# Preparing the down projection's weight factors: two raw tiles loaded a group in advance, two staging tiles

## The chip, the cores and the metric

The kernel runs on one core of a Trainium2 chip. The core has five engines that run side by side, each with its own queue of instructions that it works off in order: TensorE (PE; its weight loads, PEld, overlap its matmuls), VectorE (DVE), ScalarE (ACT), GpSimd (POOL) and SyncE (SP), which here issues nearly all DMAs. The metric is the time of one execution on the device in microseconds (us), the median of several runs.

## The reference, cut to what matters

One layer of a hybrid decoder over 1056 tokens (1024 of a prompt, 8 × 4 of samples): a norm, an input projection, two recurrent mixers (mLSTM and HGRN2) side by side, an output projection, and a SwiGLU feed-forward network with 1024 model columns and 2816 hidden ones (22 tiles of 128). All is float32.

```python
    x = x + jnp.einsum('btm,md->btd', mix, w_out)
    h2 = _rmsnorm(x, norm_ffn)
    ff = jax.nn.silu(jnp.einsum('btd,df->btf', h2, w_gate)) * jnp.einsum('btd,df->btf', h2, w_up)
    x = x + jnp.einsum('btf,fd->btd', ff, w_down)
```

The change is in how `w_down` (`wd` in the kernel) is made ready for the last line.

## The kernel before, in words

**Float32 products from rounded pieces.** TensorE multiplies rounded operands (type fp32r). So each operand is split in two: `hi` is the value rounded by a copy on ACT, `lo` is the value less `hi`, a subtraction on DVE or POOL. A product is three matmuls: hi·hi, hi·lo, lo·hi. Every weight and every activation goes through such a rounding on ACT before it can be used.

**Seven products in place of eight.** The gate-and-up stage and the down projection use Strassen's scheme in Winograd's form on 2 × 2 blocks, so sums and differences of weight blocks are formed, rounded and subtracted too.

**The stages.** Input projection with the mixers (to about 690 us), output projection and two of the 22 hidden tiles ("plain"), the gate-and-up stage over the other 20 hidden tiles (from about 760 to 1175 us, `g_step`, matmuls at L1228), the plain part of the down projection (L1492), the down projection (`d_step`, L1451), and the final norm.

**The weight preparation.** `wd_prep` runs beside the gate-and-up stage. It goes through 20 groups (`NG`); a group is a block of four hidden tiles by 256 model columns, 128 × 4 × 256 numbers, 512 KB. Per group it loads the raw block (`fload`, L1357) into the tile `fr`, which has one buffer, and makes four pieces of it. Per piece, `rnd` rounds on ACT (L1364) into the upper half of a staging tile `fh`, which has three buffers, and `rest` subtracts on DVE into its other half (L1369) and stores the whole tile to DRAM (`d_wf`, L1370): three pieces of 512 KB and one of 256 KB. Between the pieces four differences are formed on DVE in place in `fr` (L1383, L1385, L1388, L1390). The down projection later loads the finished factors from `d_wf` (`dload`, L1419); the stage's end waits for the preparation to be finished (`finish(("wd",))`).

**The order.** All queues are in the program's order, which the kernel writes out by hand. Side work is held in Python generators; `hook()` counts down each one's wait and, when it has come, lets it emit its next instructions up to its next `yield n`, which asks for n more hooks. In the gate-and-up stage a step is 24 matmuls (two halves of 12) and calls `hook()` four times. So a `yield 2` in `wd_prep` puts its next instructions two hooks, 12 matmuls, later into the queues of ACT, DVE and SP, between the work of the stage: the copies that empty PSUM on ACT (L1236, L1196), the sums on DVE (L1195, L1199, L1201), the splitting of the gate and up weights (L1145 on DVE, L1156 on ACT, L1157 on POOL), their loads (L1134) and the stores of results (L1209) on SP. An instruction that must wait for its data holds up all that stands behind it in its engine's queue.

**The hooks of one group before.** The three waits are `WDY = (2, 2, 5)`. With the group's first rounding at hook 0: second rounding and first store 2, second store 4, differences 6 and 8, third rounding and third difference 10, fourth difference 12, third store and fourth rounding 14, fourth store 16, load of the next group 18, next group's first rounding 23.

Of the kernel before, what the change touches and what calls it, by code (L numbers as in the profile page):

```python
# [9 lines left out]
F32 = mybir.dt.float32  # L10
F32R = mybir.dt.float32r
# [29 lines left out]
def hybrid_step(ctx: ExitStack, tc: tile.TileContext, i, o):  # L41
# [964 lines left out]
    fpool = [None]  # L1006
# [338 lines left out]
    NG = 4 * NS  # L1345
# [6 lines left out]
    def wd_prep():  # L1352

        def fload(g):
            t = fpool[0].tile([128, 4, 256], F32, tag="fr", name="fr", bufs=1)
            f = NPLAIN + 4 * (g // 4)
            nc.sync.dma_start(t, i["wd"].rearrange("(f p) d -> p f d", p=128)[:, f:f + 4, 256 * (g % 4):256 * (g % 4) + 256])  # L1357
            return t

        def rnd(src):  # L1360
            n = 128 * src.shape[1]
            t = fpool[0].tile([128, 1024], F32R, tag="fh", name="fh", bufs=3)
            h, lw = (x.rearrange("p (f c) -> p f c", c=128) for x in (t[:, 0:n], t[:, n:2 * n]))
            nc.scalar.activation(h, src, AF.Copy)  # L1364
            return t, h, lw, n

        def rest(g, k, src, p):
            t, h, lw, n = p
            nc.vector.tensor_tensor(lw, src, h.bitcast(F32), op=OP.subtract)  # L1369
            nc.sync.dma_start(d_wf[g, k, :, 0:2 * n], t[:, 0:2 * n].bitcast(F32))  # L1370
        r = fload(0)
        yield WDY[0]
        for g in range(NG):
            left, right = r[:, :, 0:128], r[:, :, 128:256]
            a11, a12, a21, a22 = left[:, 0:2], left[:, 2:4], right[:, 0:2], right[:, 2:4]
            p = rnd(left)
            yield WDY[1]
            rest(g, 0, left, p)
            p = rnd(a22)
            yield WDY[1]  # L1380
            rest(g, 1, a22, p)
            yield WDY[1]
            nc.vector.tensor_tensor(a22, a21, a22, op=OP.add)  # L1383
            yield WDY[1]
            nc.vector.tensor_tensor(a21, a11, a21, op=OP.subtract)  # L1385
            yield WDY[1]
            p = rnd(right)
            nc.vector.tensor_tensor(a11, a22, a11, op=OP.subtract)  # L1388
            yield WDY[1]
            nc.vector.tensor_tensor(a12, a12, a11, op=OP.subtract)  # L1390
            yield WDY[1]
            rest(g, 3, right, p)
            p = rnd(left)
            yield WDY[1]
            rest(g, 2, left, p)
            yield WDY[1]
            if g + 1 < NG:
                r = fload(g + 1)
            yield WDY[2]

    WDY = (2, 2, 5)

    def dplace(g, k):

# [283 lines left out]
    nxt = 2  # L1688
# [9 lines left out]
    for ui, u in enumerate(units + [None]):  # L1698
        if ui == units1:
            start(t3_prep(), ("t3",))  # L1700
            gi, TPK = 2, 2
            for k, (gu_, p) in enumerate(steps):
                while gi < len(groups) and gat[gi] <= k and (groups[gi][1] != 1 or (1, 0) in graw):
                    start(gsplit(*groups[gi], dve=gi < 2), ("gs", gi))
                    gi += 1
                finish(("gs", groups.index((GROUP[p], gu_))))
                if k == TPK:
                    finish(("t12",))
                if (gu_, p) == (0, "P7"):
                    finish(("tp",))  # L1710
                    finish(("t3",))
                if (gu_, p) == (1, "P1"):
                    start(wd_prep(), ("wd",))
                if (gu_, p) == (NU - 2, "P4"):
                    finish(("gs", len(groups) - 1))
                    start(plain_prep(), ("s2", 0))
                    hook()
                    load(n_t1)
                    load(n_t1 + 1)
                    for j in range(2):  # L1720
                        start(split(n_t1 + j, True), ("w", n_t1 + j), WLW[j])
                g_step(gu_, p)
                if (gu_, p) == (NU - 1, "P6"):
                    x2[0] = act.tile([128, KT, T], F32, tag="X", name="X2")
                    load_x2(0)
                    load_x2(2)
# [198 lines left out]
```

## Time and profile before

| | us |
|---|---|
| median of 3 runs | 1428.82 (1426.03 to 1429.61) |
| the profiled execution | 1429.1 |
| its span, first to last instruction | 1427.3 |
| mean granted TensorE clock | 0.98 |
| TensorE busy | 1363.0 |
| VectorE busy | 951.2 |
| GpSimd busy | 643.1 |
| ScalarE busy | 523.8 |
| bytes moved by DMA | 211.97 MB, 149 GB/s over the span |

The profile is one execution, in us from the start of its span. Rows of groups and timelines name an engine, a line of the kernel, an operation and its tiles as out<-in; in square brackets stands the time for which the engine had nothing running before that row, and what ended it. Rows of waits read "engine tile line <- what ended the wait: us in total, times, longest". Rows of windows give the busy time of each engine in a stretch with its number of instructions, then TensorE's granted clock as a share, the mean busy share of the 16 DMA engines, and GB/s. Rows of the chain give start, length and what, along the chain of work that ended last.

### The profile page before, as it was taken

What the parts mean: (1) busy time and instruction counts of PE and PEld (TensorE: products, weight loads), DVE (VectorE), ACT (ScalarE), POOL (GpSimd) and SP (SyncE); (2) the same over time, 40 slices, a digit from 0 to 9 for tenths busy, and PEclk for the clock granted to TensorE, in tenths of its full rate; (3) what the DMA queues carried; (4) which work ended last, traced back from release to release, by engine and by line L of the source; (5) the groups of instructions that cost most, each with busy time, mean ns of one, the idle gap of its engine ahead of it and who ended that gap; (6) DMA issues with size and microseconds to landing.
All of it is one profiled execution on the core that took longest, in us unless ns stands there. A gap on an engine that the chain in (4) does not pass through costs nothing. (4 is left out here: it accounts for less than half of the span.)

```text
span 1427.3 us, 27173 instructions
## 1 busy us (share of the span) xinstructions
PE 1363.0 (95%) x10384; PEld 1332.7 (93%) x10384; DVE 951.2 (67%) x2192; ACT 523.8 (37%) x1195; POOL 643.1 (45%) x648
## 2 busy tenths in 40 slices
PE   7878999999999999999998999999999999999996
PEld 6778999899999998899998999999999999999995
DVE  7876657666767677753756666665766436777776
ACT  6544334232222223322535444544444441222233
POOL 5323212234344434312537656655655684544445
PEclk8999999999999999999999999999999999999998
DMA  6012112331100113542463665665666268787843
GB/s 220 23 42 76 58 45 72 97 94 30 33 31 32 42 34 98 162 149 90 144 218 115 242 233 182 234 223 204 210 215 219 87 210 330 281 300 276 297 168 122
DMA packets 108875, 211.97 MB, mean 149 GB/s; under 512 B 10800, under 2 KB 63560, under 8 KB 108232
## 3 DMA queue, kind: packets, MB, share of 16 engines
q1 hardware_dynamic: 108312, 209.98, 43.0%
q8 instruction: 82, 1.34, 0.4%
q14 instruction: 49, 0.40, 0.1%
q10 hardware_dynamic: 432, 0.24, 0.1%
HBM read 143.73 MB, written 66.45 MB: 147 GB/s over the span
## 5 line engine op out<-in xcount | busy, mean ns | idle before, releaser
L135 PE MATMUL mm<-HI,whi 128*128 128x384 f32 (+2 forms) x1160 | 382.8, 330 | 5.4 <-ACT st L417 1.8
L137 PE MATMUL mm<-HI,wlo 128*128 128x384 f32 (+2 forms) x1160 | 363.5, 313 | 1.3 <-POOL wlo L97 1.3
L136 PE MATMUL mm<-LO,whi 128*128 128x384 f32 (+2 forms) x1160 | 363.9, 314 | 0.9 <-POOL LO L225 0.4
L135 PEld LDWEIGHTS mm<-HI,whi 128*128 128x128 f32 x1160 | 222.1, 191 | 10.7 <-ACT st L417 2.1
L136 PEld LDWEIGHTS mm<-LO,whi 128*128 128x128 f32 x1160 | 222.5, 192 | 2.1 <-POOL LO L225 0.9
L137 PEld LDWEIGHTS mm<-HI,wlo 128*128 128x128 f32 x1160 | 221.8, 191 | 1.8 <-POOL wlo L97 1.8
L97 POOL TENSOR_TENSOR wlo<-raw,whi 128x512 fp32r<-128x512 f32 x90 | 119.7, 1339 | 145.0 <-ACT whi L96 100.1
L1157 POOL TENSOR_TENSOR wlo<-S,whi 128x512 fp32r<-128x512 f32 x78 | 108.3, 1395 | 112.8 <-ACT whi L1156 95.9
L1369 DVE TENSOR_TENSOR fh<-fr,fh 128x512 fp32r<-128x512 f32 x80 | 77.3, 971 | 71.9 <-ACT fh L1364 71.3
L1228 PE MATMUL mx<-T,whi 128*128 128x264 f32 x640 | 118.5, 284 | 1.7 <-DVE sg L1195 1.7
L1228 PEld LDWEIGHTS mx<-T,whi 128*128 128x128 f32 x640 | 99.0, 188 | 2.0 <-DVE sg L1195 1.9
L1281 POOL TENSOR_TENSOR LO<-rg,HI 128x528 fp32r<-128x528 f32 x52 | 69.8, 1351 | 65.8 <-ACT HI L1280 59.5
L1228 PE MATMUL mx<-HI,whi 128*128 128x264 f32 x320 | 92.0, 287 | 4.4 <-ACT u L1236 4.4
L1228 PE MATMUL mx<-HI,wlo 128*128 128x264 f32 x320 | 91.6, 286 | 0.0
L1228 PE MATMUL mx<-LO,whi 128*128 128x264 f32 x320 | 91.4, 286 | 0.0
L1228 PE MATMUL mx<-T,wlo 128*128 128x264 f32 x320 | 90.9, 284 | 0.0
L802 POOL TENSOR_TENSOR ck<-ck,wib 128x192 f32<-128x192 f32 (+2 forms) x72 | 41.2, 572 | 100.5 <-PE mx L757 56.2
L1455 DVE TENSOR_TENSOR X<-X,mx 128x264 f32<-128x264 f32 x160 | 65.5, 425 | 26.4 <-PE mx L1451 26.0
L1156 ACT ACTIVATE whi<-S 128x512 fp32r<-128x512 f32 x80 | 50.4, 631 | 75.4 <-DVE S L1145 75.2
L1364 ACT ACTIVATE fh<-fr 128x512 fp32r<-128x512 f32 x80 | 45.2, 570 | 72.2 <-DMA fr<-in_wd 49.6
L1280 ACT ACTIVATE HI<-rg 128x528 fp32r<-128x528 f32 x52 | 32.3, 642 | 105.0 <-PE mx L1451 36.8
L1228 PE MATMUL mm<-HI,whi 128*128 128x264 f32 x240 | 68.3, 285 | 0.0
(536 smaller groups left out, 3604.0 us busy)
## 6 DMA issues: line engine op xcount, KB each, us to landing
d_wf<-fh SPq DMA_DIRECT2D x60, 512.0 KB
rg<-d_ff SPq DMA_DIRECT2D x42, 528.0 KB
raw<-in_wA SPq DMA_DIRECT2D x31, 512.0 KB
whi<-d_wf SPq DMA_DIRECT2D x29, 512.0 KB
wlo<-d_wf SPq DMA_DIRECT2D x28, 512.0 KB
raw<-in_wgu SPq DMA_DIRECT2D x24, 512.0 KB
d_ff<-sg SPq DMA_DIRECT2D x40, 264.0 KB
rg<-in_wgu SPq DMA_DIRECT2D x20, 512.0 KB
```

What stands on the lines that cost most here:

```text
L97: (nc.gpsimd if pool else nc.vector).tensor_tensor(lo[:, s], raw[:, s], hi[:, s].bitcast(F32), op=OP.subtract)
L135: nc.tensor.matmul(ps[:, :n], wh, rh[:, k, :], start=(k == 0), stop=False)
L136: nc.tensor.matmul(ps[:, :n], wh, rl[:, k, :], start=False, stop=False)
L137: nc.tensor.matmul(ps[:, :n], wl, rh[:, k, :], start=False, stop=(k == nk - 1))
L802: nc.gpsimd.tensor_tensor(ke, ke, gv[:, :, 1:2].to_broadcast([128, nb, lv]), op=OP.mult)
L1156: nc.scalar.activation(hi[:, s], t, AF.Copy)
L1157: (nc.vector if dve else nc.gpsimd).tensor_tensor(lo[:, s], t, hi[:, s].bitcast(F32), op=OP.subtract)
L1228: nc.tensor.matmul(ps[:, :QN], a[:, w], b_[:, kk, c], start=new and kk == 0 and x == 0, stop=kk == 3 and x == 2, skip_group_check=True)
L1281: (nc.vector if dve else nc.gpsimd).tensor_tensor(lw, src, h.bitcast(F32), op=OP.subtract)
L1364: nc.scalar.activation(h, src, AF.Copy)
L1369: nc.vector.tensor_tensor(lw, src, h.bitcast(F32), op=OP.subtract)
L1455: nc.vector.tensor_tensor(y, y, ps[:, :QN], op=OP.add)
```

## The change

The tile `fr` gets two buffers and `fh` two in place of three, so the memory stays the same: 4 KB per partition more for the one and less for the other. The load of the next group moves from the end of a group to behind the first piece's store. The wait that stood in front of it goes, and the last wait of a group is 6 hooks in place of 5. A group's hooks are then: first rounding 0; first store, next group's load and second rounding 2; second store 4; differences 6 and 8; third rounding 10; third store and fourth rounding 14; fourth store 16; next group's first rounding 22.

```diff
         def fload(g):
-            t = fpool[0].tile([128, 4, 256], F32, tag="fr", name="fr", bufs=1)
+            t = fpool[0].tile([128, 4, 256], F32, tag="fr", name="fr", bufs=2)
...
         def rnd(src):
             n = 128 * src.shape[1]
-            t = fpool[0].tile([128, 1024], F32R, tag="fh", name="fh", bufs=3)
+            t = fpool[0].tile([128, 1024], F32R, tag="fh", name="fh", bufs=2)
...
-        r = fload(0)
+        nxt = fload(0)
         yield WDY[0]
         for g in range(NG):
+            r = nxt
             left, right = r[:, :, 0:128], r[:, :, 128:256]
             a11, a12, a21, a22 = left[:, 0:2], left[:, 2:4], right[:, 0:2], right[:, 2:4]
             p = rnd(left)
             yield WDY[1]
             rest(g, 0, left, p)
+            if g + 1 < NG:
+                nxt = fload(g + 1)
             p = rnd(a22)
...
             rest(g, 2, left, p)
-            yield WDY[1]
-            if g + 1 < NG:
-                r = fload(g + 1)
             yield WDY[2]
 
-    WDY = (2, 2, 5)
+    WDY = (2, 2, 6)
```

## The prediction

> **What bounds the kernel now.** I read the page's first rows, then the windows of the stage that the change touches, then who waited for whom in it.
>
> ```profile
> PE 1363.0 (95%) x10384; PEld 1332.7 (93%) x10384; DVE 951.2 (67%) x2192; ACT 523.8 (37%) x1195; POOL 643.1 (45%) x648
> ```
>
> TensorE is busy in 95% of the span, so time can come only from its idle time or its clock. The windows of the gate-and-up stage, in which the weight preparation runs, and of what follows:
>
> ```profile
> 767.00:1112.00 345.00, 338.92 (x2769) 337.81 (x2768) 227.79 (x339) 160.47 (x361) 210.13 (x167) 1.00 0.61 214
> 1112.00:1175.00 63.00, 63.00 (x520) 63.00 (x519) 21.76 (x37) 27.12 (x59) 44.89 (x37) 1.00 0.41 139
> ```
>
> After the stretch's length stand the busy times of PE, PEld, DVE, ACT and POOL. While the preparation runs TensorE idles 345.00 − 338.92 = 6.08 us; in the 63 us of the same stage after it, nothing. PE's waits in 767 to 1112 us, complete, and below them ACT's two kinds of wait at the rounding (L1364) and DVE's at the subtraction behind it (L1369):
>
> ```profile
> PE mx L1228 <- ACT u L1236: 4.4, 4, 1.8
> PE mx L1228 <- DVE sg L1195: 1.7, 1, 1.7
> ```
>
> ```profile
> ACT fh L1364 <- DMA fr<-in_wd: 49.6, 13, 6.8
> ...
> ACT fh L1364 <- issue: 20.8, 8, 4.2
> ```
>
> ```profile
> DVE fh L1369 <- ACT fh L1364: 71.3, 24, 8.0
> ```
>
> Five waits of TensorE make up 4.4 + 1.7 = 6.1 us, all the idle time. None names the preparation; they name PSUM being emptied (L1236, L1195). But ACT waits 49.6 us at its rounding for the raw weights, and DVE behind it 71.3 us. How one becomes the other is seen in ACT's and then PE's instructions at 978 us:
>
> ```profile
> 978.52 0.63 ACT L1364 ACTIVATE fh<-fr 128x512 fp32r<-128x512 f32 x1 [5.81 <-DMA fr<-in_wd]
> 979.06 0.37 ACT L1236 ACTIVATE u<-mx 128x264 f32<-128x264 f32 x1
> ```
>
> ```profile
> 979.48 0.39 PE L1228 MATMUL mx<-HI,whi 128*128 128x264 f32 x1 [1.44 <-ACT u L1236]
> ```
>
> ACT stands 5.81 us at the rounding of a group's first piece; the copy that empties a PSUM bank stands behind it in the same queue, starts at 979.06, and the matmul that needs the bank starts 1.44 us late. The chain of waits shows the largest of the five whole:
>
> ```profile
> 1078.38 5.16 DMA fr<-in_wd
> ...
> 1083.64 0.10 ACT fh L1364
> ...
> 1084.18 0.61 ACT whi L1156
> 1084.79 0.29 ACT u L1236
> 1085.08 0.04 issue
> 1085.12 0.39 PE mx L1228
> ```
>
> Load, rounding, two ACT instructions queued behind it, matmul. The fifth wait (through DVE) has the longest load, the 7.89 us quoted below, and is of the same kind. There is a second price. The clock around that wait (third column from the right, behind POOL's busy time):
>
> ```profile
> 1079.60:1083.00 3.40, 3.40 (x30) 3.40 (x29) 0.22 (x1) 0.84 (x3) 1.31 (x1) 1.00 1.01 304
> 1083.00:1086.40 3.40, 1.56 (x13) 1.35 (x12) 1.68 (x3) 2.02 (x5) 1.28 (x1) 1.00 0.81 329
> 1086.40:1089.80 3.40, 3.40 (x18) 3.40 (x17) 2.94 (x7) 2.19 (x4) 2.02 (x2) 0.51 0.45 167
> 1089.80:1093.20 3.40, 3.40 (x30) 3.40 (x30) 2.35 (x4) 1.30 (x4) 3.40 (x4) 0.99 0.00 0
> ```
>
> Right after the stretch in which TensorE was busy for only 1.56 us, one stretch of 3.40 us runs at clock 0.51: 18 matmuls start where 30 do before and after it. That costs 12 × 3.40 / 30 = 1.4 us by the count, 3.40 × 0.49 = 1.7 us by the clock. I take 1.7.
>
> **The change, part by part.** *The load moves.* First the hook, in which the yields count; these are pieces of the chain:
>
> ```profile
> 1101.50 8.74 PE mx L1228 x72
> ```
>
> 72 matmuls are three steps of 24 with four hooks each, so a hook is 8.74 / 12 = 0.73 us. Before, a group's load is issued at hook 18 of a period of 23 and its first rounding comes at hook 23: 5 × 0.73 = 3.6 us. The loads took, from issue to the release of the rounding, in the chain:
>
> ```profile
> 990.66 5.77 DMA fr<-in_wd
> ...
> 1006.10 4.91 DMA fr<-in_wd
> ...
> 1057.30 7.89 DMA fr<-in_wd
> ```
>
> So 3.6 us is too short for each of these. After the change the load is issued at hook 2 (behind the store of the first piece, in front of the second rounding) for the next group's rounding at hook 22: 20 × 0.73 = 14.6 us, nearly twice the longest. The new load's own wait is for the tile that the previous group left at hook 16, eight hooks earlier, so SP stands at it for nothing. In SP's queue it comes in front of the second piece's store and of the gate weights' loads; each delay is at most its issue, 384 to 741 ns by the row of the loads below. Only the first group's load keeps its wait, and no wait of TensorE lies there. Removed: TensorE's 6.1 us and the 1.7 us of clock, together 7.8 us.
>
> *The period goes from 23 to 22 hooks.* Instructions and bytes stay the same: 80 roundings, 80 subtractions, 80 differences on DVE, 80 stores, 20 loads.
>
> ```profile
> L1357 SPq DMA_DIRECT2D fr<-in_wd x20: 384/428/741, 767.8 to 1095.6; - x20
> ```
>
> The 20 loads lie 327.8 / 19 = 17.3 us apart; 22 hooks are 16.0 us. Work is packed 8% denser: DMA's share would go from 0.61 to 0.66, DVE's from 227.79 / 345 = 0.66 to 0.71. Neither reaches its end, and the preparation ends some 20 us earlier in a stage in which TensorE is full. Cost: nothing. If that cover were gone, DVE would be late next, and ACT's 62.9 us at L1156 below would grow.
>
> *Two staging tiles in place of three.* A rounding now waits for the store of the piece two before it. The stores are handed out at hooks 2, 4, 14 and 16 of a period, and the roundings that take their tiles again come at 10, 14, 22 and 24: eight hooks later, once ten, so 8 × 0.73 = 5.8 us. Behind a rounding that waits stand the same PSUM copies as behind a load now. No view shows a wait for a store, so I bound it. One pair of stores (512 and 256 KB) with a third store behind it on SP, and the bytes moved just after:
>
> ```profile
> 840.83 1.56 SPq L1370 DMA_DIRECT2D d_wf<-fh  x2
> 842.48 0.41 SPq L1209 DMA_DIRECT2D d_ff<-sg  x1
> ```
>
> ```profile
> 843.20:844.40 1.20, 1.20 (x12) 1.20 (x12) 1.20 (x3) 0.00 (x0) 1.20 (x2) 1.00 0.97 370
> 844.40:844.80 0.40, 0.40 (x6) 0.40 (x5) 0.40 (x1) 0.00 (x0) 0.40 (x1) 1.00 0.02 5
> ```
>
> At 844.40 the queue is empty: three stores in 844.40 − 840.83 = 3.6 us. The subtraction's own lag is small when ACT is on time:
>
> ```profile
> 838.81 0.62 ACT L1364 ACTIVATE fh<-fr 128x512 fp32r<-128x512 f32 x1
> ```
>
> The subtraction's hook is two hooks later, 840.27, and SP issues at 840.83: 0.6 us. The store has landed 0.6 + 3.6 = 4.2 us after the hook, against 5.8: no wait. The other end is a store as slow as the longest load: 0.6 + 7.9 − 5.8 = 2.7 us of ACT at every rounding. What ACT's standing costs TensorE: before, 49.6 + 20.8 = 70.4 us cost 7.8, so 0.11 us each (an estimate). Ends: 0 and 80 × 2.7 × 0.11 = 24 us. I take one such store in 80, the nearest row being the 3.6: 2.7 × 0.11 = 0.3 us. With ten slow ones, where the gate weights' two loads meet the group's load in the queue, it is 3 us; that goes into the range.
>
> *What is late next.* ACT still waits in this stretch for DVE, in front of the same copies:
>
> ```profile
> ACT whi L1156 <- DVE S L1145: 62.9, 49, 3.9
> ```
>
> The rounding at 845.22 is another such wait, 2.66 us, for the preparation's own difference (L1385), which DVE ended at 845.14; it is one of the 8 put down to "issue", and stays:
>
> ```profile
> 845.22 0.64 ACT L1364 ACTIVATE fh<-fr 128x512 fp32r<-128x512 f32 x1 [2.66 <-issue]
> ```
>
> ```profile
> 843.97 1.17 DVE L1385 TENSOR_TENSOR fr<-fr 128x256 f32<-128x256 f32 x1
> ```
>
> None over 3.9 us, and TensorE has lost nothing to them alone; the next bound is TensorE itself.
>
> *Behind the stage.* Do 7.8 us at 1085 reach the end? The chain at the turn to the down projection:
>
> ```profile
> 1174.33 0.97 PE mm L1492 x6
> 1175.31 0.81 SPq L1419
> ...
> 1176.65 6.49 DMA raw<-d_wf
> ```
>
> The loads of prepared weights, through which TensorE's next wait comes, start behind the stage's last matmuls, not by a clock of their own, and the preparation was over at 1112. All that moves with TensorE.
>
> **Sum.** Against the profiled execution's 1429.1 us (span 1427.3): 1429.1 − 6.1 − 1.7 + 0.3 = 1421.6 us. The median 1428.82 lies 0.3 below that execution, so I predict 1421.3 us.
>
> **The rivals.** *The clock doesn't give back.* 18 matmuls where 30 would be is one event, its place is set by where 3.4 us stretches fall, and another shortage of TensorE (the turn at 1175 to 1240, the end) may take it in its place. Then 1421.3 + 1.7 = 1423.0 us. For it: behind the wait at 978, in which TensorE was busy for 2.25 of 3.40 us, no drop follows:
>
> ```profile
> 975.80:979.20 3.40, 2.25 (x19) 2.03 (x17) 0.02 (x1) 0.68 (x2) 0.00 (x0) 1.00 0.63 230
> 979.20:982.60 3.40, 3.12 (x25) 3.12 (x26) 3.37 (x6) 2.10 (x5) 1.38 (x2) 1.00 0.55 217
> ```
>
> Against it: the one drop that I find in 767 to 1112 lies directly behind the largest of the waits that go. The Trainium skill, TensorE: Matmul & The Clock Gate, What's actually happening, says that the clock halves after at least one idle window of about 3.4 us, on windows that run free; by that, a wait of 1.84 us would not halve it, the drop would not be this wait's, and the sum would keep the 1.7. This trace disagrees: 0.51 stands behind a stretch with 1.56 of 3.40 us busy. Chance 0.14.
>
> *The waits move.* ACT's queue still has DVE's lateness (62.9 us) and some late stores in front of PSUM copies; half of the 7.8 stays: 1421.3 + 3.9 = 1425.2 us. For it: denser DVE. Against: of five losses every one I traced had a load at its head. Chance 0.16.
>
> *Nothing comes of it*, since TensorE would be held at the same five places by DVE, whatever ACT does: 1428.8 us. For it: one of five waits names DVE. Against: DVE itself had waited for ACT's rounding, 71.3 us in all. Chance 0.06. That the load should still be late is excluded: 14.6 us against 7.89.
>
> *Slower: the two staging tiles.* Every rounding waits for a store, where a load was waited for once in a group. It breaks even when ACT stands as long as before, 70.4 us, or 0.9 us at each of 80 roundings; that is, when stores land on average later than 5.8 + 0.9 − 0.6 = 6.1 us after their issue. At 7.9 us the price is 24 − 7.8: 1421.3 − 0.3 + 24 = 1445 us. Against it: 3.6 us for three at once. Chance 0.04.
>
> **How the numbers follow.** The forecast has 0.60: 1421.3 us, with 1.7 either way for one more or one fewer stretch of half clock elsewhere, so 1419.6 to 1423.0. Runs before the change spread from 1426.03 to 1429.61, 2.8 below their median, so the range starts at 1418.5; upward it takes in ten slow stores (1424.0) and the moved waits (1425.2) and ends at 1426.0. 0.3% of 1428.82 is 4.3 us, about what a measurement of this kernel can tell from no change: faster is below 1424.5, the forecast and the clock rival, 0.74; within it the moved waits and nothing, 0.22; slower 0.04.
>
> **What would show it.** In the changed kernel ACT's wait at L1364 for the load should be left at the first group alone, PE busy should be full from 776 to about 1165, with no stretch below clock 1.00, and the stage's last matmuls should come near 1167. If ACT's wait at the rounding is as large as before with no load named, the stores hold it. The prediction fails if TensorE's waits there exceed 3 us, or if they are gone and the turn to the down projection grows by as much.

## The result and the profile after

| | before | changed | ratio (95% interval) |
|---|---|---|---|
| median, first runs, us | 1427.42 (4 runs, 1425.81 to 1429.61) | 1418.43 (4 runs, 1417.77 to 1418.89) | 0.9936 (0.9918 to 0.9953) |
| median, five more rounds, us | 1426.94 (23 runs) | 1417.02 (6 runs) | 0.9932 (0.9918 to 0.9945) |
| profiled execution, us | 1429.1 | 1418.89 | |
| its span, us | 1427.3 | 1417.1 | |

The kernel is 9 to 10 us faster. The page's first rows of the changed kernel: busy times and shares of the span.

```profile
span 1417.1 us, 27194 instructions
...
PE 1361.7 (96%) x10384; PEld 1332.4 (94%) x10384; DVE 936.4 (66%) x2192; ACT 528.8 (37%) x1195; POOL 643.8 (45%) x648
```

TensorE's busy time is nearly what it was; the span is shorter. The windows of the changed kernel beside the preparation and in the rest of the stage:

```profile
767.00:1112.00 345.00, 345.00 (x2845) 345.00 (x2844) 218.75 (x346) 169.23 (x369) 215.45 (x172) 1.00 0.62 217
1112.00:1162.00 50.00, 50.00 (x414) 50.00 (x414) 15.78 (x28) 21.12 (x45) 35.66 (x31) 1.00 0.42 140
```

TensorE is busy for all of the 345.00 us, against 338.92 before; from 767 to 1162 us it has no wait at all. The number to look at is the count in brackets: 2845 matmuls ran in the stretch, 2769 before (either count takes in the two or three that had begun just ahead of it). At 345 / 2845 = 0.121 us each, the 76 more are worth 9.2 us. ACT's waits at the rounding and DVE's behind it, in the same stretch of the changed kernel:

```profile
ACT fh L1364 <- DMA d_wf<-fh: 19.8, 12, 3.6
...
ACT fh L1364 <- DMA fr<-in_wd: 4.6, 1, 4.6
```

```profile
DVE fh L1369 <- ACT fh L1364: 33.0, 23, 7.7
```

One load is still waited for, the first group's, as foreseen. New are 12 waits for a store (d_wf<-fh), up to 3.6 us long; TensorE loses nothing to them.

Where the 10.2 us between the two profiled spans lie is read from the first matmul of the stage's tile T and the first of the plain part, the starts in these groups. Before the change:

```profile
L1228 PE MATMUL mx<-T,whi x640: 278/284/392, 765.9 to 1171.0; 128*128 128x264 f32 x160
```

```profile
L1492 PE MATMUL mm<-HI,whi x24: 320/322/325, 1174.2 to 1195.7; 128*128 128x352 f32 x24
```

And of the changed kernel:

```profile
L1228 PE MATMUL mx<-T,whi x640: 278/284/289, 763.0 to 1158.9; 128*128 128x264 f32 x160
```

```profile
L1492 PE MATMUL mm<-HI,whi x24: 320/322/325, 1162.1 to 1183.6; 128*128 128x352 f32 x24
```

Up to the stage 765.9 − 763.0 = 2.9 us less, where no instruction was changed; in it 408.3 − 399.1 = 9.2 us less; from its end to the span's end 253.1 before and 255.0 after, 1.9 us more. 2.9 + 9.2 − 1.9 = 10.2. Only the 9.2 us are the change's. The first and the last part move between executions, of one and the same kernel too: in the changed kernel's second profile the stage starts at 763.8, the plain part at 1163.0 and the span ends at 1415.4, so the last part there takes 252.4 us. Over the twelve profiles of this record, whose kernels are alike up to the stage, it starts between 761.3 and 766.2 us. The stage itself repeats: in the five profiles in which TensorE has no wait in it (the changed kernel twice and three kernels of the next section) it takes 399.1 or 399.2 us.

### The profile page after: what moved, and what is told of

The parts are those of the page before. It is cut to its first block, busy times and chain, and to the rows that moved or that the text cites. A ratio compares the mean times of both kernels' runs of the same rounds, so it can differ in the third digit from the quotient of the medians.

```text
span 1417.1 us, 27194 instructions
## 1 busy us (share of the span) xinstructions
PE 1361.7 (96%) x10384; PEld 1332.4 (94%) x10384; DVE 936.4 (66%) x2192; ACT 528.8 (37%) x1195; POOL 643.8 (45%) x648
## 4 chain that ended last, share of the span: by engine, by line
PE 50%; DVE 3%; DMA 2%; issue 1%; ACT 1%; SPq 0%; POOL 0%; POOLq 0%; DVEq 0%; ACTq 0%
PE mx L1228 16%; PE mm L1228 9%; PE mx L1451 8%; PE mm L1451 5%; PE so L1228 3%; PE mm L135 2%; PE mm L136 2%; PE mm L137 2%; DMA rg<-d_ff 1%; PE so L1451 1%; DMA raw<-d_wf 1%; PE mx L644 1%; DMA rg<-d_h 0%; DVE X L1455 0%; PE so L1555 0%
## 5 line engine op out<-in xcount | busy, mean ns | idle before, releaser
L1228 PE MATMUL mx<-T,whi 128*128 128x264 f32 x640 | 118.2, 284 | 0.0
L1228 PEld LDWEIGHTS mx<-T,whi 128*128 128x128 f32 x640 | 99.0, 188 | 0.0
L1228 PE MATMUL mx<-HI,whi 128*128 128x264 f32 x320 | 91.0, 284 | 0.0
L1228 PE MATMUL mx<-T,wlo 128*128 128x264 f32 x320 | 90.9, 284 | 0.0
L1228 PE MATMUL mx<-HI,wlo 128*128 128x264 f32 x320 | 90.9, 284 | 0.0
L1228 PE MATMUL mx<-LO,whi 128*128 128x264 f32 x320 | 90.7, 283 | 0.0
L1369 DVE TENSOR_TENSOR fh<-fr,fh 128x512 fp32r<-128x512 f32 x80 | 68.3, 853 | 33.2 <-ACT fh L1364 33.0
L1228 PE MATMUL mm<-HI,wlo 128*128 128x264 f32 x240 | 68.2, 284 | 0.0
L1228 PE MATMUL mm<-HI,whi 128*128 128x264 f32 x240 | 68.2, 284 | 0.0
```

What stands on the lines that cost most here:

```text
L1228: nc.tensor.matmul(ps[:, :QN], a[:, w], b_[:, kk, c], start=new and kk == 0 and x == 0, stop=kk == 3 and x == 2, skip_group_check=True)
```

## The experiments

**The changed kernel again, and the load alone.** The second differs from the changed kernel in the staging tiles only (two for the long pieces and a third, half as large, for the short one):

```diff
-            t = fpool[0].tile([128, 1024], F32R, tag="fh", name="fh", bufs=2)
+            tag = "fh" if n == 512 else "fh1"
+            t = fpool[0].tile([128, 2 * n], F32R, tag=tag, name=tag, bufs=2 if n == 512 else 1)
```

> The changed kernel once more, on this chip, with more rounds. Theory (the raw weights' load stood in front of PSUM copies in ScalarE's queue, five waits of TensorE in the gate-and-up stage went with it): 1418.5 us, 1417.5 to 1419.5, no wait of TensorE from 770 us to the turn to the down projection, that stage 9.1 us shorter than before (first matmul of L1228 to first matmul of L1492: 425.2 us before, 415.8 after). Rival (a part of the 9 us is a difference of executions that lies outside the stage): the stage still 415.8, but this kernel's median moves by over 1.5 us from 1418.4.

> The changed kernel with a staging tile more (two of 4 KB and one of 2 KB for the short piece, so that a tile is taken again at the earliest 12 hooks after its store is handed out): the early load alone. Theory: 1418.4 us, within 1 us of the changed kernel, since TensorE has no wait left in the stage; ACT's waits at the rounding shorter than in the changed kernel. Rival (store waits take something back): faster than the changed kernel by over 1 us, 1417 or less.

The changed kernel again took 1417.02 us, 1.4 below its first median: below the theory's range, and just short of the rival's 1.5. In the stage it has no wait, and from the first matmul of L1228 to the first of L1492 it takes 416.2 us (425.2 before, 415.8 in the first profile). So the stage's gain repeats, and what differs between the two medians lies outside it. The load alone took 1418.10 us, ratio 0.9943 (0.9927 to 0.9959). Its windows over the same stretch:

```profile
767.00:1112.00 345.00, 345.00 (x2844) 345.00 (x2843) 215.91 (x346) 168.92 (x371) 214.62 (x170) 1.00 0.62 216
```

2844 matmuls, as with two staging tiles. ACT's waits for a store there are 1.4 us in all, in place of 19.8, and TensorE gains nothing by it: the third tile would buy nothing.

**Two staging tiles alone.** The kernel before with `bufs=2` for `fh`, nothing else.

```diff
-            t = fpool[0].tile([128, 1024], F32R, tag="fh", name="fh", bufs=3)
+            t = fpool[0].tile([128, 1024], F32R, tag="fh", name="fh", bufs=2)
```

> The kernel before with two staging tiles in place of three, its load and its period as before. Theory: store waits cost nothing beside the load's wait, the loads are as late as before; 1427 us, within 2 us of before, ACT waiting some 70 us at the rounding, four to six waits of TensorE. Rival (the stores of two staging tiles hold ScalarE): 2 us or more slower, 1429 to 1451. Rival (fewer staging tiles help): 1423 or less.

1426.59 us, ratio 0.9997 (0.9984 to 1.0010): no change, four waits of TensorE. With the two runs above, the gain is the load's and none of it the staging tiles'.

**One raw tile, longer wait.** The kernel before, with the group's last wait 9 and then 7 hooks in place of 5.

```diff
-    WDY = (2, 2, 5)
+    WDY = (2, 2, 9)
```

> The kernel before with one raw tile and three staging tiles, the last wait of a group nine hooks in place of five, so that the load has 9 x 0.73 = 6.5 us and a group 27 hooks. Theory (it is the late load, not the number of tiles): the loads of 4 to 5.5 us come in time, the two or three of 6.5 to 7.9 us are late by 1 us at most; 1419.5 us, 1418 to 1421.5, at most one wait of TensorE, under 1 us. Rival (two raw tiles or the closer packing bring the gain): 1424 to 1428. Rival (a preparation that ends later, near 1155 us, is late for the down projection): slower than 1428.

```diff
-    WDY = (2, 2, 5)
+    WDY = (2, 2, 7)
```

> The kernel before with one raw tile and three staging tiles, the last wait of a group seven hooks in place of five: the load has 7 x 0.73 = 5.1 us, a group 25 hooks. Theory (late load in front of PSUM copies; and the preparation must be over before the loads of the stage's end, which begin near 1141 us): loads of 5 us come in time, three or four queued ones are late by 1 to 3 us, the preparation ends near 1135 and meets nothing; 1418 to 1422 us, none or two waits of TensorE. Rival (a longer period costs by itself, as with 27 hooks): 1423 to 1427.

With 9 hooks: 1424.63 us, ratio 0.9984 (0.9972 to 0.9995), a fifth of the gain, outside what the theory had expected and inside the range of the rival that two raw tiles or the closer packing bring the gain. Its windows and, for the whole stage, PE's waits:

```profile
767.00:1112.00 345.00, 344.98 (x2840) 344.64 (x2839) 201.43 (x327) 164.29 (x359) 212.03 (x172) 1.00 0.57 200
```

```profile
PE mx L1228 <- ACT u L1236: 4.2, 2, 2.4
```

Up to 1112 next to nothing is lost; two waits come later, where SP's queue holds the preparation's last stores in between the loads for the down projection. SP's instructions there, and ACT's first wait for one of these loads:

```profile
1149.59 0.42 SPq L1370 DMA_DIRECT2D d_wf<-fh  x1
1150.11 0.40 SPq L1209 DMA_DIRECT2D d_ff<-sg  x1
1150.55 8.68 SPq L1274 DMA_DIRECT2D rg<-d_ff  x3
1159.29 0.90 SPq L1370 DMA_DIRECT2D d_wf<-fh  x2
```

```profile
1152.14 0.65 ACT L1472 ACTIVATE HI<-rg 128x528 fp32r<-128x528 f32 x1 [4.69 <-DMA rg<-d_ff]
```

The clock pays here too; it is halved in two stretches behind the first of the two waits:

```profile
1159.60:1163.00 3.40, 1.60 (x8) 1.29 (x7) 2.33 (x3) 2.56 (x6) 3.40 (x3) 0.50 0.93 234
1163.00:1166.40 3.40, 3.40 (x17) 3.40 (x17) 0.43 (x1) 1.76 (x3) 3.40 (x4) 0.50 1.05 432
```

The preparation, 27 hooks a group, runs into the loads of the next stage; that the two late waits come from this meeting is read from the queues, not tried. With 7 hooks it hands out its last store at 1125.9 and meets nothing: 1416.85 us, ratio 0.9925 (0.9901 to 0.9949), below the 1418 to 1422 expected, with 2844 matmuls in the stretch. So one raw tile does as well as two, in the memory of the kernel before, and the rival of the two tiles or the packing falls. Yet ACT still waits long there, more than the theory had foreseen:

```profile
ACT fh L1364 <- DMA fr<-in_wd: 29.3, 9, 5.3
```

Waits of up to 5.3 us cost TensorE nothing here, while waits of 2.8 and 3.2 us (those that end at 892.68 and 1083.64 us) had cost it before. Their length doesn't settle the price. Where the remaining waits fall is left to chance, since 25 hooks of a group drift against the stage's 28; so a part of this kernel's good time may be luck.

**The load late again, and 23 hooks.** The changed kernel with its load at hook 18, and with its last wait 7.

```diff
-            if g + 1 < NG:
-                nxt = fload(g + 1)
             p = rnd(a22)
...
             rest(g, 2, left, p)
-            yield WDY[2]
+            yield WDY[1]
+            if g + 1 < NG:
+                nxt = fload(g + 1)
+            yield WDY[2] - 2
```

> The changed kernel with both pairs of tiles and 22 hooks, but the load issued at hook 18, four hooks = 2.9 us ahead of its use. Theory (the time between load and use is all that counts): loads late by 1.5 to 5 us in every group, 1427 to 1433 us, four to seven waits of TensorE in the stage. Rival (two raw tiles or the closer packing help by themselves): 1418 to 1423.

```diff
-    WDY = (2, 2, 6)
+    WDY = (2, 2, 7)
```

> The changed kernel with 23 hooks in a group as before. Theory (packing is neutral while TensorE is full and the preparation ends ahead of the next loads): within 1.5 us of the changed kernel, 1416 to 1419.5, 2840 to 2846 matmuls in 767 to 1112 us, the preparation over at about 1099 in place of 1085. Rival (closer packing costs or gives something): over 2 us away.

Late: 1433.34 us, just above the theory's range, ratio 1.0038 (1.0026 to 1.0050), so slower than before with all four tiles in place. PE's waits in 767 to 1112 us:

```profile
PE mx L1228 <- ACT u L1236: 7.5, 4, 3.7
PE mx L1228 <- DVE u L1201: 1.8, 1, 1.8
PE mx L1228 <- DVE sg L1195: 1.8, 1, 1.8
```

Six waits, 7.5 + 1.8 + 1.8 = 11.1 us. The tiles give nothing unless the load is early. 23 hooks: 1419.07 us, ratio 0.9927 (0.9903 to 0.9950), 2845 matmuls; packing is neutral.

**One staging tile.** The changed kernel with `bufs=1` for `fh`, to see what waits for stores cost.

```diff
-            t = fpool[0].tile([128, 1024], F32R, tag="fh", name="fh", bufs=2)
+            t = fpool[0].tile([128, 1024], F32R, tag="fh", name="fh", bufs=1)
```

> The changed kernel with one staging tile: a rounding waits for the store of the piece just before it. The second and the fourth rounding of a group then follow their store in the same hook and wait some 3.5 to 4.2 us each, 40 waits, 140 to 170 us of ScalarE. Theory (a store wait costs TensorE what a load wait costs, 0.11 to 0.13 us per us of ScalarE): 15 to 22 us slower than the changed kernel, 1432 to 1440 us, over ten waits of TensorE in the stage. Rival (store waits fall where TensorE has banks to spare): 1417 to 1421.

1501.28 us, ratio 1.0509 (1.0490 to 1.0527). ACT's waits for stores (in 767 to 1246 us, its longer stage) and the windows of the usual stretch:

```profile
ACT fh L1364 <- DMA d_wf<-fh: 175.4, 52, 6.0
```

```profile
767.00:1112.00 345.00, 297.23 (x2256) 293.56 (x2255) 184.40 (x281) 132.03 (x295) 165.84 (x134) 0.93 0.50 178
```

ACT's 175 us are near the 140 to 170 expected; the time is far above the theory's range and the rival's. 2845 − 2256 = 589 matmuls are lost in the stretch, 71 us, some 24 of them by the clock at 0.93 (345 × 0.07); over the whole the kernel is 84 us slower than the changed one, 0.48 us for each us of ACT, where 0.11 had been assumed.

**The same wait at two places.** The kernel before with the load one hook ahead of its use, so that every group's rounding waits, and a group of 28 hooks, the stage's own period, so that all waits meet the same place of it. The two kernels differ in the first wait only (24 or 5 hooks).

```diff
             rest(g, 2, left, p)
-            yield WDY[1]
+            yield WDY[2]
             if g + 1 < NG:
                 r = fload(g + 1)
-            yield WDY[2]
+            yield 1
...
-    WDY = (2, 2, 5)
+    WDY = (24, 2, 11)
```

> The kernel before with a load issued one hook ahead of its use, so that ScalarE waits 3.4 to 6 us at the first rounding of every group, and with 28 hooks in a group, which is the period of the gate-and-up stage itself (seven steps of four hooks): each wait meets the same place of the stage. Here that place is hook 22 after that of the first group before, where the copies of the sixth product (u<-mx) stand behind the rounding. Theory (what counts is whether that copy, whose bank the next step but one adds into, is behind the wait): over 20 us of waits of TensorE in 767 to 1112 us, fewer than 2680 matmuls started there (2845 when none waits). Rival (the length of ScalarE's wait alone counts, 0.11 us for each us): about as many as the other kernel of this pair, 2770 to 2800. The preparation ends after the stage's matmuls in both, so only this stretch is compared.

> The same with the waits at hook 3, where splitting of weights and PSUM copies with a later use stand behind the rounding. Theory (the place counts): no or one wait of TensorE in 767 to 1112 us though ScalarE waits as long at the rounding as in the other kernel, 2830 to 2845 matmuls there. Rival (the length alone counts): 2770 to 2800, as in the other.

Windows and ACT's waits at the load, first for hook 22, then for hook 3:

```profile
767.00:1112.00 345.00, 333.69 (x2720) 332.04 (x2719) 195.70 (x296) 147.72 (x332) 202.49 (x164) 1.00 0.52 182
```

```profile
ACT fh L1364 <- DMA fr<-in_wd: 45.8, 11, 6.4
ACT fh L1364 <- DMA d_ff<-sg: 14.7, 3, 5.1
```

```profile
767.00:1112.00 345.00, 345.00 (x2845) 345.00 (x2844) 213.37 (x321) 161.46 (x355) 216.37 (x171) 1.00 0.56 192
```

```profile
ACT fh L1364 <- DMA fr<-in_wd: 71.7, 17, 6.1
```

At hook 22 ACT waits 45.8 + 14.7 = 60.5 us (the three waits put down to d_ff<-sg stand at the same rounding, which reads only fr) and TensorE loses 2845 − 2720 = 125 matmuls, 15 us: less than the over 165 that the theory expected and more than the rival's 45 to 75, since TensorE had 8 waits to ACT's 14, and ACT's waits of 3.5 us and less cost nothing there either. At hook 3 ACT waits longer, 71.7 us, up to 6.1 at a time, and TensorE loses none in this stretch. The place decides. (No place is free under all circumstances: just behind the stretch, at 1122.17 us, a wait of 3.24 us at hook 3 is followed by one of TensorE of 1.00 us, put down to DVE.) ACT's and PE's instructions at one wait at hook 22:

```profile
856.62 0.63 ACT L1364 ACTIVATE fh<-fr 128x512 fp32r<-128x512 f32 x1 [6.40 <-DMA fr<-in_wd]
857.15 0.61 ACT L1156 ACTIVATE whi<-S 128x512 fp32r<-128x512 f32 x1
857.67 0.37 ACT L1236 ACTIVATE u<-mx 128x264 f32<-128x264 f32 x1
```

```profile
858.10 0.59 PE L1228 MATMUL mx<-HI,whi 128*128 128x264 f32 x1 [2.82 <-ACT u L1236]
```

TensorE's wait is 3.58 us shorter than ACT's here, and 3.85 to 3.91 us shorter at TensorE's other seven waits in the stretch; one of them:

```profile
987.43 0.63 ACT L1364 ACTIVATE fh<-fr 128x512 fp32r<-128x512 f32 x1 [6.07 <-DMA fr<-in_wd]
```

```profile
988.91 0.39 PE L1228 MATMUL mx<-HI,whi 128*128 128x264 f32 x1 [2.21 <-ACT u L1236]
```

So ACT has some 3.9 us to spare at this place: a shorter wait costs nothing, and a longer one what it has beyond that. ACT's instructions at one wait at hook 3:

```profile
895.40 0.63 ACT L1364 ACTIVATE fh<-fr 128x512 fp32r<-128x512 f32 x1 [5.46 <-DMA fr<-in_wd]
895.93 0.41 ACT L1196 ACTIVATE sg<-sg 128x264 f32<-128x264 f32 x1
```

Behind the first stands the copy of the sixth product (u<-mx). Each half of a product has a bank of its own, and the seventh adds into it after the sixth's other half and one other step, 12 + 24 = 36 matmuls or 36 × 0.121 = 4.4 us, so that copy can be little later than that. Behind the second stands an activation of finished sums, for which no matmul waits soon. (The totals of these two, 1464.97 and 1437.42 us, tell nothing of this: their preparation ends after the stage's matmuls and holds the turn to the down projection.)

## Why the prediction was right or wrong

Forecast 1421.3 us, range 1418.5 to 1426.0; measured 1418.43, just below the range, and 1417.02 in the second set. The direction and the mechanism held; a term of the sum was too small. Of the 2.9 us between forecast and measurement, 1.4 are not the sum's: the kernel before had a median of 1428.82 us in the three runs that the forecast starts from, and of 1427.42 with a fourth. The term that was too small rests on how PE's rows are read; these are the ones around the wait at 979 us before the change:

```profile
977.64 0.28 PE L1228 MATMUL mx<-LO,whi 128*128 128x264 f32 x1
977.76 0.28 PE L1228 MATMUL mx<-HI,wlo 128*128 128x264 f32 x1
979.48 0.39 PE L1228 MATMUL mx<-HI,whi 128*128 128x264 f32 x1 [1.44 <-ACT u L1236]
979.71 0.28 PE L1228 MATMUL mx<-LO,whi 128*128 128x264 f32 x1
979.83 0.28 PE L1228 MATMUL mx<-HI,wlo 128*128 128x264 f32 x1
```

- **The load holds ACT's queue, and PSUM copies stand behind it:** right. The late load brings the waits back, the early one removes them, and staging tiles, packing and period do neither.
- **6.1 us of idle time as the price of five waits:** this is the step that failed. The idle time of a busy column is not the time lost. By the counts of matmuls, the 2769 of before against 2845 are 9.2 us; less 1.7 for the clock that is 7.5 us for five waits, where the sum had 6.1: 0.28 us each on top of the idle time shown. Why can be seen in the rows above: a matmul is listed with 0.28 us but the next starts 0.12 us behind it, so idle time is counted only from 0.16 us after the start that was missed; and behind the first one after a wait, listed with 0.39 us, the next starts only after 0.23 us, 0.11 more than usual. 0.16 + 0.11 = 0.27 us a wait, as the counts have it. Had the sum gone by the pace of the 72 matmuls that it shows (8.74 / 72 = 0.1214 us), 2842 would have fitted into the 345 us, against 2767 that started there (2769 less the two begun before). That is 75 matmuls or 9.1 us, and a forecast of about 1420.0 us; with before's median of 1427.42 us, 1418.6.
- **1.7 us of clock:** right for the stage, in which no stretch runs below 1.00 after. (The 18 and 30 of the prediction each count two matmuls begun before their stretch: 16 start, 0.22 us apart, where 28 do.) The clock rival's half, that a shortage elsewhere takes it over, is not excluded: the changed kernel's profile has a halved stretch at the turn (below) and one at 1400.8 us that before's profile had not, and 1.9 us more from the turn to the end; its second profile has neither.
- **Two staging tiles:** the cost of nothing is right, for another reason than I gave. I expected one store in 80 to be late; 12 were. They cost nothing, the longest with 3.6 us, so the 0.3 us that the sum put on them was nothing; at hook 22, the worst place tried, only 8 of 14 waits reached TensorE, and those of 3.5 us and less did not. The 0.11 us per us of ACT on which the slower rival's price rested was wrong: 0 and 0.25 (15 / 60.5) at two places of the stage, 0.48 with waits twice in a group.
- **20 hooks for the load:** right, though far more than needed. 7 hooks with one tile do, even with loads that still come late.
- **The turn to the down projection moves with TensorE:** right within the 2.6 us by which that part differs between two executions of the changed kernel (255.0 and 252.4).
- **The range:** its low end was taken from the spread of before's runs and not from the sum's own error, so it had no room for a term that is too small.

## What to carry to other kernels

A late transfer costs what stands behind it in its engine's queue, so look for the copy with the nearest deadline before counting the length of a wait; only what the wait has beyond that copy's spare time is paid, here what it had beyond 3.9 us at one place, and nothing at another. Moving the wait by some instructions can be worth as much as a second buffer. Price a stall of TensorE by the matmuls that didn't start, at the rate of a full stretch next to it, not by its idle time. A side job stretched to take waits out of it must still be over before the next stage's loads begin.

## What the runs showed of the hardware that was not expected

In the gate-and-up stage, TensorE's clock halves for 3.4 us after a stretch of 3.4 us that is idle for little more than half of it. Of the 3.40 us in these pairs of rows the first had 1.69 us busy in the kernel before and 1.58 us with the two staging tiles alone:

```profile
1066.00:1069.40 3.40, 1.69 (x14) 1.48 (x13) 3.27 (x5) 1.67 (x4) 2.68 (x2) 1.00 0.53 208
1069.40:1072.80 3.40, 3.40 (x30) 3.40 (x29) 2.44 (x7) 2.02 (x5) 1.94 (x2) 1.00 0.08 28
```

```profile
973.20:976.60 3.40, 1.58 (x14) 1.37 (x12) 0.65 (x2) 1.21 (x3) 0.00 (x0) 1.00 0.45 167
976.60:980.00 3.40, 3.40 (x18) 3.40 (x17) 3.37 (x8) 1.63 (x4) 2.01 (x2) 0.51 0.59 231
```

1.71 us idle left the clock at 1.00, 1.82 us brought 0.51. In the kernel with the late load, 1.80 us idle from 872.66 to 876.07 us left it at 1.00 as well. The kernel before had its wait at this place of the stage too, at 978 us: 1.44 us, and the clock stayed at 1.00; in the kernel with two staging tiles alone it was 1.82 us, and the clock took 1.7 us more. And at the turn of the changed kernel:

```profile
1185.80:1189.20 3.40, 1.29 (x11) 1.16 (x10) 3.40 (x5) 0.64 (x1) 1.61 (x2) 1.00 0.18 30
1189.20:1192.60 3.40, 3.40 (x16) 3.12 (x16) 3.21 (x12) 1.18 (x2) 2.50 (x2) 0.50 0.96 358
```

A longer wait that was split between two stretches cost no clock. With the waits at hook 22, the wait of 2.21 us shown above lies in two of them, 1.08 us in the first and 1.13 in the second:

```profile
984.36:987.78 3.42, 2.34 (x20) 2.13 (x18) 0.00 (x0) 0.35 (x1) 0.00 (x0) 1.00 0.50 177
987.78:991.19 3.41, 2.28 (x18) 2.28 (x19) 2.67 (x4) 1.99 (x6) 1.29 (x1) 1.00 0.41 163
991.19:994.60 3.41, 3.41 (x30) 3.41 (x29) 3.39 (x5) 2.83 (x7) 2.78 (x3) 1.00 0.18 67
```

So a wait just under 2 us costs nearly the double when it falls whole into such a stretch, and nothing more when it is split. That executions of one kernel can differ by some 1.7 us for this reason follows, but was not tried. The places of the stretches are inferred from where the drops start, in steps of 3.413 us (in the kernel before two drops start at 758.76 and 1086.44 us, 96 such steps apart). Near the end of the program the limit is another: in the kernel with 7 hooks the clock drops to 0.50 at 1398.92 us, behind a stretch of 3.41 us with 2.16 us busy.
